# Recurrence gates on quarters of the TensorE array, and one batch of attention output for the last token tile

## The chip, the cores and the metric

The kernel runs on one core of a Trainium2 chip, in one launch. The metric is device time in microseconds. The kernel before was run three times: 825.77 us is the median, 825.62 the fastest and 826.32 the slowest. One more execution was profiled.

## The reference

Two layers of a decoder trunk for 256 tokens of width 1024. Each layer has a mixer, a cross-attention into 256 memory tokens and a SwiGLU feed-forward part, each followed by a norm and a residual sum. The mixer projects the tokens once and gives the columns to three groups of heads: a gated linear recurrence (RG-LRU), forgetting attention (FoX) and retention. The change touches the first two:

```python
def rg_lru(x, w_r, b_r, w_i, b_i, lam):
    xb = x.reshape(bsz, s, LRU_BLOCKS, LRU_BLOCK)            # 4 blocks of 64 channels
    r = jax.nn.sigmoid((jnp.einsum('bsni,nij->bsnj', xb, w_r).reshape(bsz, s, LRU_WIDTH) + b_r))
    i = jax.nn.sigmoid((jnp.einsum('bsni,nij->bsnj', xb, w_i).reshape(bsz, s, LRU_WIDTH) + b_i))
    log_a = -LRU_C * r * jax.nn.softplus(-lam)
    a = jnp.exp(log_a)
    u = jnp.sqrt(-jnp.expm1(2.0 * log_a)) * (i * x)
    ...
    # h[t] = a[t] * h[t-1] + u[t], by an associative scan

def forgetting_attention(q, k, v, f_logit, b_f):             # 8 heads of 64
    ...
    p = jax.nn.softmax(jnp.where(mask, logits, -jnp.inf), axis=-1)
    return jnp.einsum('bhqk,bhkd->bhqd', p, v)               # causal, blocks of 128 queries
```

## The kernel before, in words

Activations lie in two token tiles of 128, or transposed with the channels on the partitions. Large weights stream from HBM in pieces of up to 1056 columns into five raw buffers. ScalarE rounds a piece to `hi` (f32r), VectorE computes `lo = raw - hi` (in a few cases a DMA that adds does), and TensorE multiplies in three products, hi*hi, hi*lo and lo*hi (`mm3`). Eight buffers hold split pieces. Small products (gates, attention scores and outputs, retention) are plain f32 matmuls, which the profile records as two passes each.

The order of all instructions is set when the program is built. `Flow` keeps a model clock for each engine. `matmul` (lines 319 to 332) adds a matmul's modelled cost: for f32 it is 2 * max(0.112, n/1200 + 0.0025) us for n columns, halved where 64 rows or 64 output partitions are used, a quarter for 32 rows. The main thread writes the large projections. The other work is written as generators, which say what they wait for, and are resumed between two groups of matmuls once the model clock has reached that time (`flow.tick`). The same clock decides when `pump` writes the split of the next weight piece, and, between 60 and 130 us, whether its `lo` goes to a DMA. So a changed cost can change the order of everything behind it.

The recurrence (`lru`, lines 955 to 1014) works on 256 channels as two chunks `c` of 128 partitions, two blocks of 64 channels in each. `bd` holds for each layer, gate and chunk a 128x128 matrix with the two 64x64 blocks on its diagonal and zeros elsewhere. Lines 975 to 978 write four matmuls, 128x128 weights against 256 tokens: gate 0 (recurrence gate) into one PSUM bank, gate 1 (input gate) into another. Lines 979 to 982 are four tanh activations on ScalarE, to `tr` and `ti` (tiles lr and li in the profile).

The attention (`fox`, lines 888 to 941) has three units: u = 0 is the first token tile with all four pairs of heads, u = 1 and u = 2 are the second tile with two pairs each. Each unit makes scores (lg), softmax (pexp), four transposes for each half e of the pairs (tr, copied to pT), and the product with the values (fo, lines 931 to 936): 64 output channels for e = 0 on partitions 0 to 63, for e = 1 on 64 to 127, of one bank. For the second tile, u = 1 fills half of the bank's columns and u = 2 the other half, and then the bank is split to the left operand of the output projection (line 939). Retention scores (rsc) use 32 rows at a time.

`rows_product` then runs the output projection (tiles dn): first the two leading row blocks for both token tiles, then the rest of the first tile, then the rest of the second.

Of the kernel before, what the change touches and what calls it, by code (L numbers as in the profile page):

```python
# [17 lines left out]
P = 128  # L18
# [268 lines left out]
def decoder(ctx: ExitStack, tc: tile.TileContext, a, out):  # L287
# [22 lines left out]
    def small(shape, dt=F32, n="s"):  # L310
        return sp.tile(shape, dt, tag="s", name=nm(n), bufs=60)

    def bank(n="ps"):
        return pp.tile([P, 512], F32, tag="ps", name=nm(n))
# [4 lines left out]
    def matmul(out_ap, lhsT, rhs, start, stop):  # L319
        nc.tensor.matmul(out_ap, lhsT, rhs, start=start, stop=stop)  # L320
        n = _size(out_ap)
        if lhsT.dtype == F32:
            cost = 2 * max(0.112, n / 1200.0 + 0.0025)
        elif lhsT.dtype == F32R:
            cost = max(0.119, n * 0.4475e-3 + 0.0025)
        else:
            cost = n / 2400.0 + 0.0025
        if lhsT.shape[0] == HD or out_ap.shape[0] == HD:
            cost *= 0.5
        elif lhsT.shape[0] == 32:  # L330
            cost *= 0.25
        flow.issue("PE", cost * flow.slow(), [out_ap], [lhsT, rhs])
# [31 lines left out]
    def split(hi, lo, src, later=None):  # L364

        def low(eng=V):
            eng.tensor_tensor(lo, src, hi, op=ALU.subtract)

        S.copy(hi, src)
        if later is None:  # L370
            low()
        else:
            later.append(low)
# [19 lines left out]
    def quads(ap):  # L393
        return ap.rearrange("p (c i) -> p c i", c=4)
# [406 lines left out]
    def mixer(l, xt, blk, skew, between=None):  # L801
# [81 lines left out]
                for i in range(3):  # L883
                    flow.spawn(fox(i))

        fo, mx, rsum, ri = {}, *([small([P, 8], n=n) for _ in range(NT)] for n in ("mx", "rsum", "ri"))

        def fox(u):

            t, js = ((0, range(4)), (1, range(0, 2)), (1, range(2, 4)))[u]  # L890
            w, n = P * (t + 1), len(js)
            while u > 0 and not got.get(("fox", u - 1)):
                yield 0.3
            yield qT + kT
            bs = [bank("lg") for _ in range(2)]
            for i, j in enumerate(js):
                for e in range(2):
                    r = slice(64 * e, 64 * e + 64)
                    matmul(bs[e][:, i * w:(i + 1) * w], qT[j // 2][r, j % 2, t * P:(t + 1) * P],
                           kT[j // 2][r, j % 2, 0:w], True, True)  # L900
            ps = []
            for e in range(2):
                yield bs[e]
                p, o = work([P, 512], n="pexp"), 4 * e + js[0]
                ps.append(p)
                pv, bv = (x.rearrange("p (j k) -> p j k", j=n) for x in (p, bs[e]))
                V.scalar_tensor_tensor(pv, bv, xt[t].by[HD ** -0.5], far[e, u], op0=ALU.mult, op1=ALU.add)
                V.tensor_reduce(mx[t][:, o:o + n], pv, axis=AX, op=ALU.max, negate=True)
            for e in range(2):
                p, o = ps[e], 4 * e + js[0]  # L910
                yield mx[t][:, o:o + n]
                got["fox", u] = e
                for i in range(n):
                    S.activation(p[:, i * w:(i + 1) * w], p[:, i * w:(i + 1) * w], AF.Exp,
                                 bias=mx[t][:, o + i:o + i + 1], scale=1.0, accum_out=rsum[t][:, o + i:o + i + 1])
            for e in range(2):
                p, o = ps[e], 4 * e + js[0]
                yield p
                V.reciprocal(ri[t][:, o:o + n], rsum[t][:, o:o + n])
                pv = p.rearrange("p (j k) -> p j k", j=n)  # L920
                V.tensor_tensor(pv, pv, ri[t][:, o:o + n].unsqueeze(2).to_broadcast([P, n, w]), op=ALU.mult)
            pT = []
            for e in range(2):
                yield ps[e]
                tb = transposes([ps[e][:, j * P:(j + 1) * P] for j in range(4)])
                pT.append(work([P, 4, P], n="pT"))
                S.copy(pT[e], quads(tb))
            yield pT
            if t not in fo:
                fo[t] = bank("fo")  # L930
            for i, j in enumerate(js):
                for kt in range(t + 1):
                    for e in range(2):
                        o = (2 * j + e) * HD
                        matmul(fo[t][64 * e:64 * e + 64, j * P:(j + 1) * P], v[kt][:, o:o + HD],
                               pT[e][:, i * (t + 1) + kt, :], kt == 0, kt == t)
            got["fv", u] = 1
            if u != 1:
                split(mt[t][0][:, 2:6, :], mt[t][1][:, 2:6, :], quads(fo[t]))
                for k in range(2, 6):  # L940
                    got["mt", t, k] = 1

        lxp, lyT = [None], [None]

# [10 lines left out]
        def lru():  # L955
            x, ly = lxp[0], lyT[0]
            xc, g = work([P, 2, SEQ], n="xc"), work([P, 2, SEQ], n="lg")
            tr, ti = work([P, 2, SEQ], n="lr"), work([P, 2, SEQ], n="li")

            S.activation(g, ly, AF.Square, bias=0.0, scale=1.0)  # L960
            for c in range(2):
                def cw(j):
                    o = L_CW + 8 * l + 2 * j + c
                    return cols[:, o:o + 1]
                ob = L_CB + 2 * l + c
                V.tensor_scalar(xc[:, c, :], x[:, c, 3:3 + SEQ], cw(3), cols[:, ob:ob + 1], op0=ALU.mult, op1=ALU.add)
                for j in range(3):
                    V.scalar_tensor_tensor(xc[:, c, :], x[:, c, j:j + SEQ], cw(j), xc[:, c, :], op0=ALU.mult,
                                           op1=ALU.add)
                yield 1.0  # L970
            PO.tensor_scalar(g, g, 0.044715, 1.0, op0=ALU.mult, op1=ALU.add)
            V.tensor_tensor(g, g, ly, op=ALU.mult)
            yield xc
            yield MARGIN - 1.0
            bg = [bank("gate") for _ in range(2)]
            for gate, b in enumerate(bg):
                for c in range(2):
                    matmul(b[:, c * SEQ:(c + 1) * SEQ], bd[:, l, gate, c, :], xc[:, c, :], True, True)
            for gate, dst, b in ((0, tr, bg[0]), (1, ti, bg[1])):
                for c in range(2):  # L980
                    o = 4 * gate + 2 * l + c
                    S.activation(dst[:, c, :], b[:, c * SEQ:(c + 1) * SEQ], AF.Tanh, bias=hb[:, o:o + 1], scale=0.5)
            yield [tr, ti]
            S.activation(g, g, AF.Tanh, bias=0.0, scale=float(np.sqrt(2.0 / np.pi)))
            t2, r = work([P, 2, SEQ], n="t2"), work([P, 2, SEQ], n="rec")
            for c in range(2):
                f, f2 = (x[:, 2 * l + c:2 * l + c + 1] for x in (sp2, sp4))
                S.activation(t2[:, c, :], tr[:, c, :], AF.Tanh, bias=f, scale=f)
                S.activation(r[:, c, :], tr[:, c, :], AF.Exp, bias=f2, scale=f2)
            yield t2  # L990
            S.activation(tr, t2, AF.Sqrt, bias=0.0, scale=-1.0)


            d = work([P, 2, SEQ], n="ld")
            PO.tensor_scalar(d, t2, 1.0, -1.0, op0=ALU.mult, op1=ALU.add)
            PO.tensor_scalar(r, r, 0.5, 0.5, op0=ALU.mult, op1=ALU.add)
            V.tensor_tensor(d, d, r, op=ALU.mult)
            u, h = ti, d
            V.scalar_tensor_tensor(u, ti, 1.0, xc, op0=ALU.add, op1=ALU.mult)
            yield [d, tr]  # L1000
            V.scalar_tensor_tensor(r, d, 2.0, r, op0=ALU.add, op1=ALU.mult)
            V.tensor_tensor(u, u, tr, op=ALU.mult)
            V.scalar_tensor_tensor(t2, t2, 1.0, r, op0=ALU.add, op1=ALU.mult)
            V.tensor_tensor(u, u, r, op=ALU.mult)
            yield u
            for c in range(2):
                V.tensor_tensor_scan(h[:, c, :], t2[:, c, :], u[:, c, :], 0.0, op0=ALU.mult, op1=ALU.add)
            V.scalar_tensor_tensor(g, g, 1.0, ly, op0=ALU.add, op1=ALU.mult)
            yield [g, h]
            V.scalar_tensor_tensor(h, h, 0.5, g, op0=ALU.mult, op1=ALU.mult)  # L1010
            yield h
            for t in range(NT):
                split(mt[t][0][:, 0:2, :], mt[t][1][:, 0:2, :], h[:, :, t * P:(t + 1) * P])
                got["mt", t, 0] = got["mt", t, 1] = 1
# [359 lines left out]
```

## Time and profile before

| what | value |
|---|---|
| median of three runs | 825.77 us |
| lowest and highest | 825.62, 826.32 us |
| the profiled execution, its own time | 826.53 us |
| its span, first to last instruction | 824.6 us |
| granted TensorE clock, mean | 0.998 |
| TensorE busy | 815.6 us |
| VectorE, ScalarE, GpSimd busy | 584.6, 453.4, 94.4 us |
| HBM read | 151.59 MB, 185 GB/s over the span |

In the lines of the profile, PE is TensorE's matmuls, PEld its weight loads, DVE VectorE, ACT ScalarE, POOL GpSimd, and L320 is line 320 of the kernel. A timeline line is: start, duration, engine, line, operation, tiles out<-in, shape (128*64 is rows times columns of the array used, then partitions x elements written), count. Matmuls overlap, so the distance of their starts measures them, not their durations; a count above one means that neighbours with the same tiles were put together. A line of waits is: who waited, for whom, us in total, times, longest. A line of the chain is: start, us, what. A line of windows is: stretch, its length, then busy time (and count) of PE, PEld, DVE, ACT and POOL, the granted clock, the DMA share and GB/s.

### The profile page before, as it was taken

The page shows a single profiled execution, that of the slowest core. Times are in us where ns is not written, and L with a number is a line of the kernel's source. Part 1 is how long each engine was busy: PE and PEld are TensorE (multiplying, and loading weights), DVE is VectorE, ACT ScalarE, POOL GpSimd, SP SyncE. Part 2 cuts the span into 40 slices and gives each one's busy share as a digit, 9 for nine tenths or more (in the row PEclk, how much of TensorE's full clock was granted, in tenths as well). Part 3 has the DMA queues.
Part 4 walks back from the last instruction along what each step waited for, and adds up shares of the span by engine and source line. Part 5 has one row for each costly group of instructions (what it writes and reads, how often), then busy time and mean ns, then how long its engine had stood idle before and what let it go on. Part 6 is the DMA issues. An engine that isn't in the chain of part 4 may idle for free.

```text
span 824.6 us, 12992 instructions
## 1 busy us (share of the span) xinstructions
PE 815.6 (99%) x5011; PEld 714.8 (87%) x5011; DVE 584.6 (71%) x847; ACT 453.4 (55%) x732; POOL 94.4 (11%) x154
## 2 busy tenths in 40 slices
PE   9999999999999999999999999999999999999996
PEld 6999978998888888888889998789988888888885
DVE  6588886866577756758678878776757775867663
ACT  5577794745465544645473376555455563544541
POOL 5635010200020000000060400010002000000000
PEclk9999999999999999999999999999999999999999
DMA  8899585564357756657449773636444775747411
GB/s 289 280 299 243 186 233 167 184 216 125 113 179 243 235 162 195 202 155 233 128 133 302 163 232 121 189 117 228 151 130 130 239 225 175 224 135 248 138 48 51
DMA packets 106349, 153.49 MB, mean 186 GB/s; under 512 B 5280, under 2 KB 81968, under 8 KB 106160
## 3 DMA queue, kind: packets, MB, share of 16 engines
q1 hardware_dynamic: 99040, 138.17, 52.9%
q0 software_dynamic: 6544, 13.91, 6.8%
q8 instruction: 39, 0.64, 0.3%
q10 hardware_dynamic: 704, 0.59, 0.2%
q14 instruction: 22, 0.18, 0.1%
HBM read 151.59 MB, written 1.06 MB: 185 GB/s over the span
## 4 chain that ended last, share of the span: by engine, by line
PE 96%; issue 1%; DMA 1%; DVE 1%; ACT 0%; DVEq 0%; POOLq 0%; POOL 0%; ACTq 0%
PE acc L320 62%; PE dn L320 25%; PE tr L341 3%; PE clg L320 1%; PE co L320 1%; PE lg L320 1%; PE fo L320 1%; PE warm L320 1%; DMA raw<-in_w_down 1%; PE ry L320 1%; PE gate L320 0%; PE rsc L320 0%; ACT hi L242 0%; PE rsb L320 0%; DVE lo L242 0%
## 5 line engine op out<-in xcount | busy, mean ns | idle before, releaser
L242 DVE TENSOR_TENSOR lo<-raw,hi 128x1024 fp32r<-128x1024 f32 (+2 forms) x242 | 289.9, 1217 | 86.4 <-ACT hi L242 85.2
L320 PE MATMUL acc<-xt,hi 128*128 128x256 f32 (+1 forms) x1344 | 340.2, 332 | 0.0
L242 ACT CAST hi<-raw 128x1024 fp32r<-128x1024 f32 (+2 forms) x246 | 252.2, 1042 | 88.3 <-PE acc L320 61.4
L320 PE MATMUL acc<-xt,lo 128*128 128x256 f32 x960 | 259.1, 282 | 0.0
L320 PEld LDWEIGHTS acc<-xt,hi 128*128 128x128 f32 x1344 | 223.5, 189 | 20.6 <-issue 0.4
L320 PEld LDWEIGHTS acc<-xt,lo 128*128 128x128 f32 x960 | 181.4, 189 | 6.3
L320 PE MATMUL acc<-hi,xt 128*128 128x512 f32 (+2 forms) x320 | 83.7, 352 | 0.0
L242 POOL TENSOR_TENSOR rp<-ssp,mh 128x1 f32<-128x1 f32 x12 | 6.8, 563 | 541.8 <-DVE ssp L242 541.8
L320 PEld LDWEIGHTS acc<-hi,xt 128*128 128x128 f32 x320 | 56.1, 188 | 8.6 <-ACT hi L242 0.7
L320 PE MATMUL acc<-lo,xt 128*128 128x512 f32 (+2 forms) x160 | 54.1, 349 | 0.0
L320 PE MATMUL dn<-hi,mth 128*128 128x512 f32 x128 | 51.9, 405 | 0.0
L320 PE MATMUL dn<-hi,mtl 128*128 128x512 f32 x128 | 50.6, 395 | 0.0
L242 DVE TENSOR_TENSOR fs<-acc,fs 128x256 f32<-128x256 f32 x72 | 30.1, 419 | 28.7 <-ACT fs L242 28.7
L320 PE MATMUL dn<-lo,mth 128*128 128x512 f32 x128 | 50.4, 394 | 0.0
L242 ACT COPY fs<-acc 128x256 f32<-128x256 f32 x72 | 26.2, 364 | 37.8 <-PE acc L320 37.8
L320 PE MATMUL acc<-mem,hi 128*128 128x256 f32 x256 | 46.9, 284 | 0.0
L320 PE MATMUL dn<-hi,gh 128*128 128x512 f32 x112 | 44.4, 396 | 0.0
L320 PE MATMUL dn<-hi,gl 128*128 128x512 f32 x112 | 44.2, 394 | 0.0
L320 PE MATMUL dn<-lo,gh 128*128 128x512 f32 x112 | 44.1, 394 | 0.0
L320 PE MATMUL acc<-hi,mem 128*128 128x512 f32 x128 | 43.8, 400 | 0.0
L320 PEld LDWEIGHTS acc<-mem,hi 128*128 128x128 f32 x256 | 39.6, 189 | 1.1 <-issue 0.7
L242 DVE TENSOR_TENSOR y<-dn,gpost 128x512 f32<-128x512 f32 x24 | 16.4, 686 | 32.4 <-ACT junk L242 32.4
(207 smaller groups left out, 1185.5 us busy)
## 6 DMA issues: line engine op xcount, KB each, us to landing
raw<-in_w_gate SPq DMA_DIRECT2D x44, 512.0 KB, 4.6
raw<-in_w_up SPq DMA_DIRECT2D x44, 512.0 KB, 4.7
raw<-in_w_down SPq DMA_DIRECT2D x44, 512.0 KB, 4.7
raw<-in_w_in SPq DMA_DIRECT2D x42, 512.0 KB, 5.4
raw<-in_w_ck SPq DMA_DIRECT2D x16, 512.0 KB, 5.3
raw<-in_w_cv SPq DMA_DIRECT2D x16, 512.0 KB, 5.0
raw<-in_w_out SPq DMA_DIRECT2D x16, 512.0 KB, 4.1
raw<-in_w_cq SPq DMA_DIRECT2D x16, 512.0 KB, 4.4
```

What stands on the lines that cost most here:

```text
L242: fn(*args, **kw)
L320: nc.tensor.matmul(out_ap, lhsT, rhs, start=start, stop=stop)
L341: nc.tensor.transpose(out_ap, src, ident[0:k, 0:k])
```

## The change

The gates become eight matmuls of 64x64 weights, which leaves out the zero blocks. For one chunk, the two halves `e` of gate 0 take rows and output columns (e, e), those of gate 1 rows e and output columns 1 - e, so that the input gate's two halves lie in PSUM on exchanged sides. The loop over chunks is now the outer one. Each half of the input gate has its own activation over 64 partitions, which puts it back on its side. In `fox`, unit u = 1 stops after its transposes; u = 2 writes the output matmuls of both. The planner's cost of a matmul with 64 rows and 64 output partitions is a quarter of the full one.

```diff
--- before.py
+++ after.py
@@ -326,7 +326,7 @@
         else:
             cost = n / 2400.0 + 0.0025
         if lhsT.shape[0] == HD or out_ap.shape[0] == HD:
-            cost *= 0.5
+            cost *= 0.25 if lhsT.shape[0] == out_ap.shape[0] else 0.5
         elif lhsT.shape[0] == 32:
             cost *= 0.25
         flow.issue("PE", cost * flow.slow(), [out_ap], [lhsT, rhs])
@@ -883,7 +883,7 @@
                 for i in range(3):
                     flow.spawn(fox(i))
 
-        fo, mx, rsum, ri = {}, *([small([P, 8], n=n) for _ in range(NT)] for n in ("mx", "rsum", "ri"))
+        pTs, mx, rsum, ri = [], *([small([P, 8], n=n) for _ in range(NT)] for n in ("mx", "rsum", "ri"))
 
         def fox(u):
 
@@ -925,20 +925,22 @@
                 tb = transposes([ps[e][:, j * P:(j + 1) * P] for j in range(4)])
                 pT.append(work([P, 4, P], n="pT"))
                 S.copy(pT[e], quads(tb))
+            pTs.append((t, js, pT))
+            if u == 1:
+                return
             yield pT
-            if t not in fo:
-                fo[t] = bank("fo")
-            for i, j in enumerate(js):
-                for kt in range(t + 1):
-                    for e in range(2):
-                        o = (2 * j + e) * HD
-                        matmul(fo[t][64 * e:64 * e + 64, j * P:(j + 1) * P], v[kt][:, o:o + HD],
-                               pT[e][:, i * (t + 1) + kt, :], kt == 0, kt == t)
-            got["fv", u] = 1
-            if u != 1:
-                split(mt[t][0][:, 2:6, :], mt[t][1][:, 2:6, :], quads(fo[t]))
-                for k in range(2, 6):
-                    got["mt", t, k] = 1
+            fo = bank("fo")
+            for s, js, pT in pTs:
+                if s == t:
+                    for i, j in enumerate(js):
+                        for kt in range(t + 1):
+                            for e in range(2):
+                                o = (2 * j + e) * HD
+                                matmul(fo[64 * e:64 * e + 64, j * P:(j + 1) * P], v[kt][:, o:o + HD],
+                                       pT[e][:, i * (t + 1) + kt, :], kt == 0, kt == t)
+            split(mt[t][0][:, 2:6, :], mt[t][1][:, 2:6, :], quads(fo))
+            for k in range(2, 6):
+                got["mt", t, k] = 1
 
         lxp, lyT = [None], [None]
 
@@ -973,13 +975,19 @@
             yield xc
             yield MARGIN - 1.0
             bg = [bank("gate") for _ in range(2)]
-            for gate, b in enumerate(bg):
-                for c in range(2):
-                    matmul(b[:, c * SEQ:(c + 1) * SEQ], bd[:, l, gate, c, :], xc[:, c, :], True, True)
-            for gate, dst, b in ((0, tr, bg[0]), (1, ti, bg[1])):
-                for c in range(2):
-                    o = 4 * gate + 2 * l + c
-                    S.activation(dst[:, c, :], b[:, c * SEQ:(c + 1) * SEQ], AF.Tanh, bias=hb[:, o:o + 1], scale=0.5)
+
+            rows = [slice(HD * e, HD * e + HD) for e in range(2)]
+            for c in range(2):
+                for gate, b in enumerate(bg):
+                    for e in range(2):
+                        matmul(half(b, c)[rows[e ^ gate]], bd[rows[e], l, gate, c, HD * e:HD * e + HD], xc[rows[e], c, :],
+                               True, True)
+            for c in range(2):
+                S.activation(tr[:, c, :], half(bg[0], c), AF.Tanh, bias=hb[:, 2 * l + c:2 * l + c + 1], scale=0.5)
+            for c in range(2):
+                for e in range(2):
+                    o = 4 + 2 * l + c
+                    S.activation(ti[rows[e], c, :], half(bg[1], c)[rows[e ^ 1]], AF.Tanh, bias=hb[rows[e], o:o + 1], scale=0.5)
             yield [tr, ti]
             S.activation(g, g, AF.Tanh, bias=0.0, scale=float(np.sqrt(2.0 / np.pi)))
             t2, r = work([P, 2, SEQ], n="t2"), work([P, 2, SEQ], n="rec")
```

## The prediction

> **What bounds the kernel now.** I read the page first: its first lines, then the chain that ended last, then the waits of TensorE and of the engines that feed it, and last the timeline around the three blocks of small matmuls that the change touches.
>
> ```profile
> span 824.6 us, 12992 instructions
> PE 815.6 (99%) x5011; PEld 714.8 (87%) x5011; DVE 584.6 (71%) x847; ACT 453.4 (55%) x732; POOL 94.4 (11%) x154
> PE 96%; issue 1%; DMA 1%; DVE 1%; ACT 0%; DVEq 0%; POOLq 0%; POOL 0%; ACTq 0%
> PE warm L320 <- DVE warm L242: 1.2, 1, 1.2
> PE rsb L320 <- issue: 1.1, 1, 1.1
> PE tr L341 <- DVE fg L242: 0.2, 1, 0.2
> ACT hi L242 <- PE acc L320: 61.4, 80, 5.9
> ```
>
> A busy share of 99% would not prove much alone, since a matmul that stands in a queue can look busy. The chain says more: 96% of the span is TensorE following itself. The three lines that begin with PE are its whole table of waits (total, count, longest): 2.5 us in 825. The last line is the other side: ScalarE's casts of the weights waited 61.4 us for TensorE. So supply waits for TensorE and not the reverse, and a microsecond taken from TensorE's own stream should move the end by a microsecond, as long as the supply keeps its lead.
>
> **The gate matmuls, as they are.** Each layer has four f32 matmuls of 128x128 weights and 256 columns. The profile records two passes for each.
>
> ```profile
> 73.01 0.28 PE L320 MATMUL acc<-xt,lo 128*128 128x256 f32 x1
> 73.36 0.28 PE L320 MATMUL acc<-xt,lo 128*128 128x256 f32 x1
> 73.48 1.89 PE L320 MATMUL gate<-xc,cst 128*128 128x256 f32 x8
> 75.02 0.59 PE L320 MATMUL acc<-xt,hi 128*128 128x256 f32 x2
> 75.45 0.29 PE L320 MATMUL acc<-xt,lo 128*128 128x256 f32 x1
> 73.65 1.73 PE gate L320 x8
> ```
>
> The starts are the measure, because the durations overlap. A triple of acc matmuls takes 73.36 - 73.01 = 0.35 us. From the lo matmul at 73.36 to the next at 75.45 is 2.09 us, in which lie one such triple and the gate block: 2.09 - 0.35 = 1.74 us. The last line, from the chain, says the same (1.73). Eight passes in 1.73 us are 0.216 us a pass: they run one after another.
>
> **The gates on quarters.** Afterwards eight matmuls of 64x64 weights do this work, sixteen passes of 256 columns. In each group of four, the recurrence gate's halves use rows and columns 0 to 63 and 64 to 127, and the input gate's halves the other two quarters, which is why its outputs change sides. No 64x64 matmul is in the trace. The nearest rows are matmuls on half the rows (lg) and on a quarter of the rows (rsc).
>
> ```profile
> 97.96 0.28 PE L320 MATMUL acc<-mem,lo 128*128 128x256 f32 x1
> 98.31 0.28 PE L320 MATMUL acc<-mem,lo 128*128 128x256 f32 x1
> 98.52 1.14 PE L320 MATMUL lg<-kT,qT 64*128 64x256 f32 x8
> 99.94 0.28 PE L320 MATMUL acc<-mem,lo 128*128 128x256 f32 x1
> 58.94 0.29 PE L320 MATMUL acc<-xt,lo 128*128 128x256 f32 x1
> 59.30 0.28 PE L320 MATMUL acc<-xt,lo 128*128 128x256 f32 x1
> 59.51 1.59 PE L320 MATMUL rsc<-rot,rot 32*128 32x256 f32 x32
> 61.37 0.28 PE L320 MATMUL acc<-xt,lo 128*128 128x256 f32 x1
> ```
>
> The lg block: 99.94 - 98.31 = 1.63, less a triple of 0.35, is 1.28 us for eight passes of 256 columns. In turn they would need 8 x 0.216 = 1.73, so two run at once: four rounds of 0.216 (0.86 us), and 0.42 us to get into and out of the narrower shape. The rsc block: 61.37 - 59.30 = 2.07, less 0.36, is 1.71 us. Its 32 passes are sixteen of 256 and sixteen of 128 columns; by fours that is 4 x 0.216 + 4 x 0.108 = 1.30, and again 0.41 over. So up to four small matmuls do run together, and going in and out costs 0.4 us however many they are.
>
> The quarters are four at a time for four rounds: 0.86 + 0.42 = 1.28 us a layer, against 1.74. That takes off 0.46 a layer, 0.92 in both. The bounds: with no cost at the edges 0.86 (a gain of 1.76 in both); all sixteen passes in turn, 16 x 0.216 + 0.42 = 3.88 (a loss of 4.28). I take 1.28, since both shapes that the trace has, split by rows, run as many at once as they have tiles, and the fo block below, split by columns, does too.
>
> The Trainium skill, page "TensorEngine Tiling (Array Packing)", section "Gotcha 1: PSUM Pressure", says that different row tiles cannot access one PSUM bank at the same time. It speaks against the change: lg and rsc give each row tile a bank of its own, while in the new code both row halves of one gate write that gate's bank, though other partitions of it. By that rule the sum would be the second rival's. No row of before settles it.
>
> **The attention output in one batch.** For the second token tile, the output matmuls (fo, 128 rows by 64 columns) came in two blocks, each of sixteen passes of 128 columns, two at once. Now they are one block of thirty-two.
>
> ```profile
> 121.80 0.40 PE L320 MATMUL dn<-lo,mth 128*128 128x512 f32 x1
> 122.03 0.40 PE L320 MATMUL dn<-hi,mtl 128*128 128x512 f32 x1
> 122.36 1.09 PE L320 MATMUL fo<-pT,fv 128*64 128x128 f32 x16
> 123.80 0.48 PE L320 MATMUL dn<-hi,mth 128*128 128x512 f32 x1
> 124.11 0.40 PE L320 MATMUL dn<-lo,mth 128*128 128x512 f32 x1
> 119.91 0.44 PE tr L341 x4
> 518.33 0.39 PE L320 MATMUL acc<-lo,mem 128*128 128x512 f32 x1
> 518.56 0.40 PE L320 MATMUL acc<-hi,mem 128*128 128x512 f32 x1
> 518.89 1.09 PE L320 MATMUL fo<-pT,fv 128*64 128x128 f32 x16
> 520.26 0.39 PE L320 MATMUL acc<-lo,mem 128*128 128x512 f32 x1
> 129.01 9.94 PE dn L320 x42
> ```
>
> In the first layer, 124.11 - 122.03 = 2.08 us hold two dn matmuls (0.23 each, the distance of the first two lines), four transposes (0.44, from the chain) and the block: 1.18 us. Eight rounds of 0.108 are 0.86, so 0.32 is spent at the edges. In the second layer, 520.26 - 518.56 = 1.70 less two matmuls of 0.23 is 1.24, and 0.38 at the edges. One block in place of two pays the edges once: 0.32 + 0.38 = 0.70 us less. The rounds themselves remain. The bounds are 0 (if the edges came from the operands and not from the shape) and 0.84 (twice the 0.42 of lg).
>
> Nobody waits for the batch. Behind it come its cast on ScalarE and its subtraction on VectorE, as before, while TensorE has 9.94 us of dn matmuls (the last line) that begin with the first token tile. What the batch holds longer is two transposed buffers of the early half, about 5.5 us (122.36 to the last block), and it takes its PSUM bank that much later. No wait of TensorE on a buffer is in the table.
>
> **ScalarE.** The input gate's two activations over 128 partitions become four over 64.
>
> ```profile
> 75.45 0.84 ACT L242 ACTIVATE lr<-gate,hb 128x256 f32<-128x256 f32 x2
> 76.17 0.84 ACT L242 ACTIVATE li<-gate,hb 128x256 f32<-128x256 f32 x2
> 75.00:90.00 15.00, 15.00 (x127) 14.94 (x125) 11.84 (x19) 14.67 (x28) 3.06 (x5) 1.00 0.83 214
> 120.00:135.00 15.00, 15.00 (x94) 11.90 (x92) 8.12 (x10) 7.64 (x12) 0.00 (x0) 1.00 0.81 241
> ```
>
> Two take 76.17 - 75.45 = 0.72 us. The length of a row stays 256, so I count each of the new ones as a whole one: 0.72 us more a layer; if the cost went by partitions it would be nothing. In the first layer it falls into a full stretch (ScalarE, the fourth engine in the row, is busy 14.67 of 15 us from 75 to 90), and pushes the weight casts queued behind it. I cost it at nothing: from 120 to 135 ScalarE is busy for only 7.64 of 15, so the lag is made up there, and no weight makes TensorE wait today. If that cover were gone, it would cost up to 0.72 a layer. The new order (both gates for one half of the channels first) lets the first activation start before the block has ended.
>
> **The sum.** -0.92 - 0.70 = -1.62 us. The profiled execution took 826.53 us, its span 824.6 us; I expect a span of about 823.0 there. Against the median of 825.77 that execution was 0.76 slow, so the sum goes to the median: 825.77 - 1.62 = 824.15 us. What a measurement of this kernel can tell from no change is about 0.2%, 1.65 us: the forecast is, by 0.03 us, on that line.
>
> **The rivals.** First, the order of the program. The kernel's own planner places every later instruction by its model clock. It now books 0.86 us for a gate block (eight times a quarter of 0.43, line 323) where it booked 1.73, and its VectorE, ScalarE and weight decisions all look at that clock. Everything behind the first gate may be ordered anew. The profile has the price of a wait that was not covered: the rsb line's 1.1 us. One new wait of that kind gives -1.62 + 1.1 = -0.5, 825.3 us; the change turns slower by 0.2% only with over 3.3 us of them. For it: small blocks sit between dependent steps all over. Against it: the table shows just three waits in a program full of such blocks.
>
> Second, the quarters run two at a time, because the two row halves of a gate get in each other's way at their bank: eight rounds, 1.73 + 0.42 = 2.15 us, 0.41 more a layer than now, +0.82 - 0.70 = +0.12, 825.9 us. This is what the skill's page would have. Against it: fo has two matmuls in one bank on different partitions at once; but they are column tiles.
>
> Third, on the slower side: the queue lets no matmul pass one that is held, and the pairs that collide hold those that don't. All sixteen passes go in turn: 3.88 us, 2.14 more a layer, +4.28 - 0.70 = +3.58, 829.35 us. It decides from a gate block of 2.92 us on (2 x 1.18 - 0.70 = 1.66 lost). Against it: every matmul of lg and rsc has a second pass on the same rows as its first, and the matmuls behind it in the program ran abreast all the same.
>
> Fourth, the merged block saves nothing: -0.92, 824.85 us.
>
> **How the numbers follow.** The forecast, with its terms off by a few tenths, has 0.62; as it sits on the line I give 0.38 of that to faster and 0.24 to the same. The new order has 0.18 (0.14 the same, 0.04 slower), two at a time 0.09, all in turn 0.06, the useless merge 0.05. Faster 0.38, same 0.24 + 0.14 + 0.09 + 0.05 = 0.52, slower 0.10. The low end is both terms at their best, -1.76 - 0.70 = -2.46, 823.3. The high end takes in two at a time and half a microsecond of new waits, 826.4; the slow cases lie outside.
>
> **What would show it.** In the changed profile the gate block should have sixteen records of 64*64, starting in fours, about 1.3 us between its neighbours: right at 1.2 to 1.4, the second rival at 2.1, the third at 3.9. There should be two fo blocks a layer, the second of 32 records and near 2.1 us, with 0.7 us less for all fo. TensorE's table of waits should be no longer than three lines and 2.5 us. The prediction is wrong in its cause if the gate block is near 1.3 and the span has still not fallen by 1.6: then the table of waits names what took it.

## The result, and the profile after

The changed kernel is slower: 830.43 us median (829.5 to 831.2, 4 runs) against 825.97 us (825.62 to 826.32), a ratio of 1.0052 with a 95% interval of 1.0041 to 1.0064. That is 4.5 us lost where 1.6 us were forecast to be gained, and outside the range. The profiled execution took 831.2 us.

The first lines of the page and the start of the chain, which stood at 824.6 us, 99% and 96% before:

```profile
span 829.3 us, 13041 instructions
PE 816.5 (98%) x5027; PEld 713.3 (86%) x5027; DVE 580.8 (70%) x844; ACT 458.7 (55%) x739; POOL 99.0 (12%) x157
PE 83%; DMA 4%; issue 4%; POOL 3%; DVE 3%; ACT 2%; POOLq 0%; DVEq 0%; ACTq 0%
```

TensorE's share of the chain fell from 96% to 83%. DMA, waits for nothing visible (issue), POOL and VectorE took its place, and POOL has three instructions more (157, before 154). First, though, the two blocks that were to gain. The timeline of TensorE around the gates of the second layer and the merged block of the first:

```profile
481.91 0.28 PE L320 MATMUL acc<-xt,lo 128*128 128x256 f32 x1
482.12 1.09 PE L320 MATMUL gate<-xc,cst 64*64 64x256 f32 x16
...
483.48 0.27 PE L320 MATMUL acc<-xt,lo 128*128 128x256 f32 x1
...
128.98 0.40 PE L320 MATMUL dn<-hi,mtl 128*128 128x512 f32 x1
129.31 1.97 PE L320 MATMUL fo<-pT,fv 128*64 128x128 f32 x32
...
131.54 0.39 PE L320 MATMUL dn<-lo,mth 128*128 128x512 f32 x1
```

Of the two blocks before, the prediction shows the first. The second:

```profile
127.59 0.40 PE L320 MATMUL dn<-hi,mtl 128*128 128x512 f32 x1
127.91 1.09 PE L320 MATMUL fo<-pT,fv 128*64 128x128 f32 x16
...
129.28 0.39 PE L320 MATMUL dn<-lo,mth 128*128 128x512 f32 x1
```

The gates: 483.48 - 481.91 = 1.57, less a triple of 0.35, is 1.22 us (forecast 1.28, before 1.74). The merged block: 131.54 - 128.98 = 2.56, less two dn matmuls of 0.23, is 2.10 us (forecast 1.72 for the rounds and 0.35 for the edges, 2.07). The two blocks before took 1.18 and 129.28 - 127.59 - 2 x 0.23 = 1.23 us. Both changes did what was forecast. In the second layer the gain also arrives. Its mixer lies between the first gate start and the group of 48 acc matmuls behind the output projection, in these lines of the two chains, before and after:

```profile
477.54 1.73 PE gate L320 x8
...
548.91 5.71 PE acc L320 x48
```

```profile
150.47 5.70 PE acc L320 x48
...
482.19 1.02 PE gate L320 x16
...
552.68 5.71 PE acc L320 x48
```

548.91 - 477.54 = 71.37 us before, 552.68 - 482.19 = 70.49 after: 0.88 us less, where half of the forecast sum is 0.81. The first layer has the loss: the group that began at 145.38 before (the same line of its chain) begins at 150.47, 5.1 us later. TensorE's table of waits and the windows there show it:

```profile
PE acc L320 <- DMA lo<-in_w_cv: 2.9, 1, 2.9
PE rsb L320 <- issue: 1.5, 1, 1.5
PE warm L320 <- DVE warm L242: 1.2, 1, 1.2
PE tr L341 <- DVE fg L242: 0.2, 1, 0.2
```

```profile
103.00:107.00 4.00, 1.05 (x8) 0.77 (x7) 3.90 (x8) 4.00 (x10) 1.21 (x1) 1.00 1.08 301
107.00:111.00 4.00, 4.00 (x16) 2.39 (x16) 1.48 (x4) 0.22 (x2) 0.00 (x0) 0.59 1.08 279
```

The first line is new. TensorE waits 2.9 us for a low part of w_cv, and that part is not VectorE's: a DMA adds it. Behind the wait the granted clock (the third number from the end) is 0.59 over 4 us, which is 3.3 us at half speed (the same view from 108 to 110 us gives 0.50). The Trainium skill, page "TensorE: Matmul & The Clock Gate", section "Part 1: The HAM clock gate (the "warmup" mystery)", puts at about 3.4 us both the idle time after which the clock is halved and the busy time after which it is full again. Here a wait of 2.9 us was enough, and the way back took 3.3.

So the planner now gives other pieces of weights to the DMA. The issues by line, of before and then after, with the median us to landing last:

```profile
lo<-in_w_out POOLq DMA_DIRECT2D x3, 512.0 KB, 9.3
...
lo<-in_w_in POOLq DMA_DIRECT2D x1, 512.0 KB, 9.2
```

```profile
lo<-in_w_cv POOLq DMA_DIRECT2D x3, 512.0 KB, 12.5
...
lo<-in_w_out POOLq DMA_DIRECT2D x2, 512.0 KB, 8.7
...
lo<-in_w_ck POOLq DMA_DIRECT2D x1, 512.0 KB, 5.9
```

The one piece of w_in stays in both.

And the chain of the changed kernel between 89 and 117 us, with start, duration and what:

```profile
89.08 1.07 ACT lo L242
...
91.32 1.10 POOL gpost L237
...
96.34 7.83 issue
...
104.19 11.49 DMA lo<-in_w_cv
115.72 0.73 PE acc L320 x2
```

The last low part of w_cv is issued at 104.19 and lands 11.49 us later; TensorE goes on at 115.72. In the kernel before VectorE had the four low parts of this block of w_cv ready 6.0 to 10.9 us ahead of their first use (worked out by matching the splits in order to the matmuls that read them). The three transfers took 12.5, 15.5 and 11.5 us from issue to landing, and cannot keep that. A piece given to the DMA also costs ScalarE one copy more (ACT lo, 1.07 us). ScalarE was busy for 4.00 of 4.00 us from 103 to 107, and the copy for the last of these pieces ran only at 102.77, just before the issue at 104.19.

### The profile page after: what moved, and what is told of

It is laid out like the page before. It is cut to its first block, busy times and chain, and to the rows that moved or that the text cites. A ratio compares the mean times of both kernels' runs of the same rounds, so it can differ in the third digit from the quotient of the medians.

```text
span 829.3 us, 13041 instructions
## 1 busy us (share of the span) xinstructions
PE 816.5 (98%) x5027; PEld 713.3 (86%) x5027; DVE 580.8 (70%) x844; ACT 458.7 (55%) x739; POOL 99.0 (12%) x157
## 3 DMA queue, kind: packets, MB, share of 16 engines
HBM read 153.16 MB, written 1.06 MB: 186 GB/s over the span
## 4 chain that ended last, share of the span: by engine, by line
PE 83%; DMA 4%; issue 4%; POOL 3%; DVE 3%; ACT 2%; POOLq 0%; DVEq 0%; ACTq 0%
PE acc L320 51%; PE dn L320 25%; DMA raw<-in_w_in 2%; PE tr L341 2%; POOL ang L242 2%; DMA lo<-in_w_cv 1%; PE clg L320 1%; PE co L320 1%; ACT hi L242 1%; DVE lo L242 1%; PE fo L320 1%; DMA raw<-in_w_down 1%; DVE xc L242 0%; PE lg L320 0%; DVE soft L242 0%
## 5 line engine op out<-in xcount | busy, mean ns | idle before, releaser
L242 DVE TENSOR_TENSOR lo<-raw,hi 128x1024 fp32r<-128x1024 f32 (+1 forms) x239 | 286.2, 1216 | 89.6 <-ACT hi L242 88.8
```

What stands on the lines that cost most here:

```text
L242: fn(*args, **kw)
```

## The experiments

Theory A: the new matmuls gained what was forecast, and the pieces of w_cv whose low part a DMA adds lost it and more. Rival B: the loss comes with the new instructions, the batch, ScalarE's two more activations a layer, or the new order as a whole. In the edits, pieces of weights go by their number in the planner's list: 24 is w_in, 28 w_ck, 30 to 33 w_cv, 34 to 37 w_out. The planner's own choice was (24, 34, 35, 37) before and (24, 28, 30, 31, 33, 35, 36) after.

**The change with the old choice of pieces.**

```diff
-            if ADD_FROM < flow.now < ADD_TO and c["DVE"] > c["PE"] + DVE_LATE and lead >= ADD_LEAD and c["POOL"] < c["PE"] + 4.0:
+            if at["split"] in (24, 34, 35, 37):
```

> The changed kernel, whole, but the low parts that a DMA adds are those of the kernel before: one piece of w_in and three of w_out, none of w_ck and w_cv. Theory A (the loss is the wait for a DMA-added low part of w_cv, with the clock that it costs; the matmuls gained what was forecast): no wait of TensorE on a DMA-added low part, about 825.97 - 1.62 = 824.3 us. Rival B (the loss comes with the new instructions themselves or with the new order as a whole, whoever adds the low parts): it stays at 829 to 831 us.

Measured: 824.45 us (823.52 to 825.38, 10 runs) against 826.1; ratio 0.9978 (0.9969 to 0.9987). Its waits of TensorE:

```profile
PE warm L320 <- DVE warm L242: 1.2, 1, 1.2
PE rsb L320 <- PE acc L320: 0.9, 1, 0.9
PE tr L341 <- DMA x<-in_x: 0.2, 1, 0.2
```

All three lie ahead of the gates or at the start, none is on a weight. The same instructions without the DMA-added w_cv gain 1.65 us, and the choice of pieces is worth 830.43 - 824.45 = 6.0 us. Rival B in its general form falls: all the new instructions are there, and the loss is not.

**The kernel before with the new choice.**

```diff
-            if ADD_FROM < flow.now < ADD_TO and c["DVE"] > c["PE"] + DVE_LATE and lead >= ADD_LEAD and c["POOL"] < c["PE"] + 4.0:
+            if at["split"] in (24, 28, 30, 31, 33, 35, 36):
```

> The kernel before, with none of the new matmuls or activations, but the low parts that a DMA adds are those of the changed kernel: one piece of w_in, one of w_ck, three of w_cv and two of w_out. Theory A: the wait and the half clock come without the change, about 825.97 + 5.5 = 831.5 us, and at least 829. Rival B: 826 us, within 0.5 us of the kernel before.

Measured: 830.4 us (829.5 to 831.02), ratio 1.0049 (1.0036 to 1.0062). The loss comes with no new matmul in the kernel. It is 4.3 us, not the 5.5 expected, and in its profile the waits are shorter and the granted clock stays at 1.00:

```profile
PE acc L320 <- DVE mtl L242: 1.5, 1, 1.5
...
PE acc L320 <- ACT mkTh L242: 0.8, 1, 0.8
```

```profile
107.00:111.00 4.00, 2.50 (x20) 1.69 (x16) 2.12 (x5) 2.62 (x5) 0.00 (x0) 1.00 1.10 271
```

The waiting matmuls are those that read low parts of w_cv, at the same place in the block. ACT mkTh and DVE mtl are only the latest events that the profile found; these matmuls read neither. The first two adds were issued at 93.07 and 95.19 and took 12.0 and 14.8 us, so they landed at 105.1 and 110.0; the waiting matmuls start at 105.25 and 110.05. That the time is as long without the half clock asks what the half clock costs at all; the filled kernel below answers it.

**The two parts alone.** The batch without the gates is the `fox` half of the diff, the planner's choice of pieces being the old one by itself. The gates without the batch are the rest of it, with the old choice written in as above.

> The kernel before with the attention output of the last token tile in one batch and nothing else of the change. Theory A: one pair of block edges less a layer, 0.70 us less, about 825.3 us. Rival B, if the loss came with the batch (its later bank, its longer held buffers): 827 us or more.

> The kernel before with the gates on quarters, their four input gate activations and the planner's new cost, without the batch; the DMA-added low parts are those of the kernel before. Theory A: 0.92 us less, about 825.05 us. Rival B, if the loss came with the gates (ScalarE's two more activations a layer, or the planner's earlier clock): 827 us or more.

Measured: the batch alone 825.69 us, ratio 0.9993 (0.9984 to 1.0002); the gates alone 825.34 us, ratio 0.9989 (0.9980 to 0.9998). That is 0.4 and 0.8 us of gain, against 0.70 and 0.92 expected, and no loss in either. The gain of the batch alone cannot be told from no change by its interval; what it saved is read from the blocks in the timeline.

**The planner's cost line as it was**, with all the new instructions:

```diff
-            cost *= 0.25 if lhsT.shape[0] == out_ap.shape[0] else 0.5
+            cost *= 0.5
```

> The changed kernel with the planner's cost line as before: a gate block is booked at 1.73 us again, all instructions are the new ones. The planner then has a DMA add one piece of w_cv (not three), one of w_in and three of w_out. Theory A: the gains of 1.6 us stay, and one late low part of w_cv costs something between nothing and 3 us: 824.5 to 827.5. If the number of new instructions were the cause, or the new order in general, about 830.

Measured: 826.77 us (825.33 to 827.53), ratio 1.0004 (0.9995 to 1.0013). The software queue, through which the DMA-added parts go, moved 14.44 MB, where before it was 13.91: one piece more, of w_cv. TensorE's waits have two lines that the first experiment does not have:

```profile
PE tr L341 <- DVE yc L242: 0.8, 1, 0.8
PE dn L320 <- DMA lo<-in_w_out: 0.8, 1, 0.8
```

It did not wait for the piece of w_cv, but for one of w_out that was queued later. 2.3 us lie between this kernel and the first experiment; the two waits are 1.6 of them, and the wait of rsb, 1.4 against 0.9, is 0.5 more.

**The clock alone**: the kernel before, all its instructions, with the planner's clock set back where the new cost does so.

```diff
                     matmul(b[:, c * SEQ:(c + 1) * SEQ], bd[:, l, gate, c, :], xc[:, c, :], True, True)
+            flow.clock["PE"] -= 0.8633
```

> The kernel before, every instruction of it, but the planner's clock of TensorE is set back by 0.86 us behind each gate block, as the new cost does. One piece of w_cv more is then added by a DMA. Theory A: no gain and some loss, 826.1 to 828.5. If the clock's shift did nothing by itself: 826.1.

Measured: 826.57 us, ratio 1.0007 (0.9998 to 1.0016). It too took one piece of w_cv more (14.44 MB) and has a new wait of 1.1 us for a low part of w_out, but the time cannot be told from no change, so this run does not decide between the two. The booked cost by itself moves the choice by one piece, and so do the new instructions by themselves; only together do they make it three pieces of w_cv and 4.5 us.

**Is the half clock part of the loss?** Four matmuls that only fill the time stand where TensorE waited:

```diff
         q = bank("acc")
+        if b is blks[0]["cv", 0] and not at.get("filled"):
+            at["filled"] = True
+            for _ in range(4):
+                nc.tensor.matmul(q, ident, cst[:, C_DEC:C_DEC + 512], start=True, stop=True)
         for k in range(KC):
```

> The changed kernel, with four f32 matmuls of 512 columns (3.4 us, into the bank that the next product overwrites, so no result changes) in the place where TensorE waited 2.95 us for the first DMA-added low part of w_cv. They keep TensorE busy there, so its clock should not be halved behind the wait. If the wait and the half clock add up (3.41 us at half, 1.7 us), it falls by 1.7 us to about 828.7. If the last low part to land sets the time (issued at 104.2, landed 11.5 us later), TensorE only waits for that one instead, and it stays at 829.5 to 831.

Measured: 830.24 us (829.79 to 831.72), ratio 1.0052 (1.0039 to 1.0064): no change against the changed kernel. The timeline shows the fill, and then a wait for the second low part in place of the first; the windows show that the granted clock now stays at 1.00; the chain shows which transfer it is:

```profile
103.30 3.60 PE L523 MATMUL acc<-cst 128*128 128x512 f32 x8
...
109.71 0.47 PE L320 MATMUL acc<-hi,mem 128*128 128x512 f32 x1
111.45 0.50 PE L320 MATMUL acc<-lo,mem 128*128 128x512 f32 x1 [1.26 <-DMA lo<-in_w_cv]
```

```profile
107.00:111.00 4.00, 3.18 (x19) 2.00 (x17) 1.39 (x4) 1.03 (x4) 0.00 (x0) 1.00 1.09 278
```

```profile
96.05 15.35 DMA lo<-in_w_cv
```

The third low part, issued at 104.00, took 11.3 us and so landed at 115.3; the matmul that reads it starts at 115.34, where in the changed kernel it starts at 115.72. In the changed kernel the half clock only made TensorE arrive later at low parts that had not landed anyway. The landing sets the time; the wait and the slow clock are where it shows.

**Which pieces?** Two more edits of the same line: in one the choice is (24, 28, 35, 36), the new one without w_cv, and in the other there is none at all.

> The changed kernel, with the pieces that a DMA adds as it chose them, but for the three of w_cv, which VectorE subtracts: one of w_in, one of w_ck, two of w_out stay. If the pieces of w_cv alone are the cause: 824 to 825 us. If the piece of w_ck (with the gain row of the norm, the first in the queue) is a part of it: 826 or more.

> The changed kernel with no low part added by a DMA at all: VectorE subtracts every piece. If VectorE has the room, 824 to 824.5 us, the best of all; if it is the bound from 75 to 120 us once more pieces fall to it, TensorE waits for a subtraction and it is 825.5 or more.

Measured: 824.58 us, ratio 0.9982 (0.9973 to 0.9991), and 824.83 us, ratio 0.9984 (0.9975 to 0.9993). The second is not the best of all, as was expected for the case that VectorE has the room, but its interval overlaps that of the first. So the loss goes when the pieces of w_cv go, the piece of w_ck costs nothing by itself, and VectorE has room for all pieces. Whether the pieces of w_cv would cost as much without the piece of w_ck ahead of them in the queue was not tested. Then the kernel before without any:

> The kernel before with no low part added by a DMA. If VectorE has room for all of them, as in the changed kernel without them, 826 us, the same; if the four pieces were a relief that it needed, 827 or more.

Measured: 826.29 us, ratio 1.0000 (0.9991 to 1.0009). Letting a DMA add low parts, which lost the time, gains nothing that these runs can tell in either kernel. The changed kernel with the old choice, without the pieces of w_cv, and without any added piece beats the kernel before by 1.3 to 1.7 us, and the changed kernel as the planner ordered it by 5.6 to 6.0.

**The exchanged sides.** The input gate on the same quarters as the recurrence gate, with the pieces of the first experiment:

```diff
-                        matmul(half(b, c)[rows[e ^ gate]], bd[rows[e], l, gate, c, HD * e:HD * e + HD], xc[rows[e], c, :],
+                        matmul(half(b, c)[rows[e]], bd[rows[e], l, gate, c, HD * e:HD * e + HD], xc[rows[e], c, :],
...
-                for e in range(2):
-                    o = 4 + 2 * l + c
-                    S.activation(ti[rows[e], c, :], half(bg[1], c)[rows[e ^ 1]], AF.Tanh, bias=hb[rows[e], o:o + 1], scale=0.5)
+                o = 4 + 2 * l + c
+                S.activation(ti[:, c, :], half(bg[1], c), AF.Tanh, bias=hb[:, o:o + 1], scale=0.5)
```

> The changed kernel with the DMA-added pieces of the kernel before, and the input gate's halves on the same quarters as the recurrence gate's (rows and columns 0 to 63, and 64 to 127), so that its two activations cover 128 partitions again. If matmuls on different quarters run together and those on one quarter in turn, the gate block is eight rounds of 0.216 and 0.42 at its edges, 2.15 us and 0.87 more a layer than on four quarters: 824.45 + 1.74 = 826.2 us. If two matmuls of one bank on different row halves held each other up, as in the second rival, sixteen rounds, 3.9 us a block and 829.6.

Measured: 826.29 us, ratio 1.0003 (0.9994 to 1.0012), 1.84 us more than with the sides exchanged. Its timeline:

```profile
73.04 0.28 PE L320 MATMUL acc<-xt,lo 128*128 128x256 f32 x1
73.40 0.28 PE L320 MATMUL acc<-xt,lo 128*128 128x256 f32 x1
73.61 1.94 PE L320 MATMUL gate<-xc,cst 64*64 64x256 f32 x16
...
75.83 0.28 PE L320 MATMUL acc<-xt,lo 128*128 128x256 f32 x1
```

75.83 - 73.40 = 2.43, less 0.36, is 2.07 us: eight rounds of two. On four quarters the same sixteen passes take 1.22. The exchange of sides is what the gates' gain consists of; without it quarters are worse than whole matrices (1.74), by the edges.

## Why the prediction was wrong

**The terms of the sum were right.** Gates: 0.46 a layer forecast, 1.74 - 1.22 = 0.52 measured. Batch: 0.70 forecast for both layers, and in the first layer 1.18 + 1.23 - 2.10 = 0.31 measured, where 0.32 was forecast. Free of the new choice of pieces, the whole change is 1.65 us faster (the first experiment), where 1.62 was forecast. The interval there goes from 1.1 to 2.6 us, so that the two agree to 0.03 is luck; that the blocks in the timeline gained what was forecast is not.

**The second and third rival are refuted.** Sixteen passes of 0.216 us by twos would take 1.73 us without any edges, so a block of 1.22 us needs four at a time: both row halves of a gate wrote one bank at once, on different partitions. The rule that the prediction quotes from the Trainium skill, page "TensorEngine Tiling (Array Packing)", section "Gotcha 1: PSUM Pressure", does not hold for this case; what held each other up here were matmuls on the same quarter (2.07 us).

**The step that failed is the first rival, its price and its chance.** The prediction saw that the planner would book 0.86 us where it had booked 1.73, and that "its VectorE, ScalarE and weight decisions all look at that clock". It then priced what may follow by the one wait in the table, 1.1 us, and gave the case 0.18, of which 0.04 slower. What came was 6.0 us, by another kind of wait: TensorE waited for transfers that the old order did not have. The code has two decisions that compare VectorE's clock with TensorE's: whether a piece is split ahead of need, and whether its low part goes to a DMA. The second acts between 60 and 130 us, and the first gate lies at 73.5. An earlier TensorE clock makes VectorE look later, so more pieces pass the test. The price stood in the profile of before, which was not asked for it: a DMA-added part takes 9.3 us to land. The planner itself (lines 172 to 176 of the kernel before) books 2.8 us in the queue and 3.0 us more until it lands, 5.8 in all on an empty queue. The single piece of w_cv took 5.9 in the run with the old cost line, the three of the changed kernel 11.5 to 15.5. The windows of ScalarE were read for whether it recovers by 120 us, and not for what is needed in between: ScalarE was already busy for 14.67 us of the 15 from 75 to 90 us, and every piece given to a DMA asks it for one copy more.

**The cover was misread.** "No weight makes TensorE wait today" was true of the order that was there. The supply's lead belongs to an order, and the change rewrote the order. With it went the cover of the term that was put at nothing, ScalarE's two activations more a layer. It was also too small. The lines show li and what follows it, in the kernel before with the new choice and then in the changed kernel:

```profile
76.61 0.84 ACT L242 ACTIVATE li<-gate,hb 128x256 f32<-128x256 f32 x2
77.32 1.16 ACT L242 ACTIVATE xg<-tr,cst 128x128 f32<-128x128 f32 x4
```

```profile
76.69 1.92 ACT L242 ACTIVATE li<-gate,hb 64x256 f32<-64x256 f32 x4
78.63 1.14 ACT L242 ACTIVATE xg<-tr,cst 128x128 f32<-128x128 f32 x4
```

Two took 77.32 - 76.61 = 0.71 us, four take 78.63 - 76.69 = 1.94: 1.23 us more, not 0.72. With the old choice of pieces it was covered, as the first experiment shows by its gain.

**The price.** Between the first experiment and the changed kernel lie 6.0 us. The kernel before loses 4.3 us to the same choice. The rest fits the views of w_cv, of the changed kernel and then of the kernel before with the new choice (the last numbers are the first and last start):

```profile
L237 POOL DMA_DIRECT2D lo<-in_w_cv x3: 1196/1197/1207, 94.1 to 104.2; - x3
```

```profile
L237 POOL DMA_DIRECT2D lo<-in_w_cv x3: 1196/1197/1207, 93.1 to 103.1; - x3
```

Since landing sets the time in the first layer, the gain of its gates, which lie ahead, is swallowed (0.5 us) and 1 us more is lost. The issue comes 1.1 us later with the new instructions, and ScalarE's added activations account for it: ScalarE begins the gates' activations at 75.88 and 75.83 us in the two kernels, is 1.31 us behind at xg, and then runs the same instructions in the same order, still 1.06 us behind at the copy for the first piece of w_cv (91.72 and 92.78). No run takes these activations out with the new choice of pieces.

## What to carry to other kernels

When a planner's clock orders the program, a change of a cost is a change of the order of all that follows. Look for the decisions in the code that compare that clock with another, work out which way they move, and price each by the slowest thing it can choose; here that was a transfer of 11.5 to 15.5 us against a lead of 6.0 to 10.9. To separate the worth of an edit from that of the order, pin the decisions (here, a list of pieces) and measure both; and try whether the device that the planner chooses (here, the adding DMA) is worth anything at all.

Quarters of the array paid here only when matmuls that follow each other directly used all four of them (1.22 us, against 2.07 on two quarters and 1.74 with whole matrices). The edges of a block of small matmuls, 0.3 to 0.4 us in these traces, were paid once for each block, so putting two blocks of one shape together saved 0.31 us in the first layer.

## What the runs showed that I had not expected

The more low parts a DMA adds in this stretch, the longer they and the plain loads beside them take to land. The lines of the DMA view from 90 to 117 us, of before and of after (packets, MB and share of the queue; count, size and median us to landing of the loads):

```profile
q0 software_dynamic: 259, 0.96, 19.6%
...
raw<-in_w_out SPq DMA_DIRECT2D x8, 512.0 KB, 4.3
```

```profile
q0 software_dynamic: 1498, 2.66, 52.4%
...
raw<-in_w_out SPq DMA_DIRECT2D x8, 512.0 KB, 9.2
```

With five adds and a gain row in the software queue instead of three adds, the loads of w_out took 9.2 us to land instead of 4.3, and one add 15.5 us. The other choices in the changed kernel fit: 3.9 us for the same loads with no add at all, 4.3 with the old choice, and 5.7 with the new choice less w_cv.

The half clock of 3.3 us cost nothing in this kernel, since TensorE had to wait for a later transfer in any case.
